# A hybrid decoder layer on one core: the first products of the up-projection put into a written order, with the norm of the second token half among them

## The chip, the core and the metric

The kernel runs on one core of a Trainium2 chip. Times are device microseconds (us) of one execution; lower is better. The engines are TensorE (PE, matrix products, with PEld for its weight loads), VectorE (DVE), ScalarE (ACT), GpSimd (POOL) and SyncE (SP, which issues every transfer here).

## What is computed

One step of a decoder layer: a mixer of Mamba-2 heads and sliding-window attention, then a convolutional feed-forward block. 1024 prompt tokens and 32 sample tokens go through the same weights, 1056 tokens in all. The part at issue is the feed-forward block:

```python
x = x + jnp.concatenate([y_ssd, y_att], axis=-1) @ lp['w_out']
hn = rmsnorm(x, lp['norm2'])
u, ffn_conv_new = causal_dwconv(hn @ lp['w_up'], ffn_conv_prev, lp['ffn_conv_w'], lp['ffn_conv_b'])
gate, val = jnp.split(u, 2, axis=-1)
x = x + (jax.nn.silu(gate) * val) @ lp['w_down']
```

with 1024 model columns, 2 x 2816 columns of `w_up` and a convolution over three tokens. `rmsnorm` scales each token by one over the root of its mean square.

## The kernel before

All operands of TensorE are split: a value is a high part (rounded, written by ScalarE with `act.activation(... Copy)`) and a low part (what the rounding left, written by VectorE as a subtraction), and a product takes high x high, high x low and low x high.

**Stages.** Input projection, mixers and the output projection come first (to 478 us of the profiled execution). The up-projection follows (478 to 949 us), then the down-projection. The up-projection's weights come in 22 pairs of 128 columns (a gate and a value block). Its tokens are two halves of 528 (`HT`), each of two quarters of 264 (`QC`).

**Seven products instead of eight.** For a pair and a half, `product(n, cp, tp, j)` with j = 0 to 6 makes the 2 x 2 block product by a seven-product scheme. `n` is a weight set, `cp` the pair, `tp` the half; j names which weight operand and which token operand it takes (`USES`: A11 with B11, S1 with T1, S2 with T2, A12 with B21, S4 with B22, S3 with T3, A22 with T4). One product is 12 matmuls of 128x264: four blocks of the contraction, three split terms each. A group is the seven products of one pair and half.

**Banks.** A group holds three PSUM banks, `bankof = "XZXYZXX"[j]`. X carries products 0, 2, 5 and 6 in a running sum, and each is read out before the next is added: 0, 2 and 6 by ScalarE, 5 by VectorE (`both(ub, ...)`, L996). So product 6 can't start before VectorE has read product 5. VectorE also reads products 3 (L1010) and 4 (L996).

**Token operands.** After the output projection of a half, `half_done` sums squares (`ssum`). `half_prep(tp)` calls `half_rstd`: twelve small matmuls with a column of ones (L851; six in the program, each in two passes), a Newton square root of fourteen tiny VectorE steps, six transposes (L858) and two ScalarE copies (L860). Then VectorE scales the half's eight blocks (L870, eight of 528 columns), forms differences (L887), and ScalarE and VectorE write seven operands, high (L882) and low (L883). B11 and T1 are needed first.

**Weight operands.** `up_load(n)` loads two raw tiles of 512 KB for weight set `n`; the pool has only two such tiles, so it waits until set n-1 is used up. `up_operand(n, j)` forms the weight operands: sums and differences (L922, L924, on VectorE for n < 3, on GpSimd from set 3 on), a high part (L934) and a low part (L935). There are eight operand tiles, so an operand of set n waits for a product of set n-1.

**Convolution.** `conv(cp, i)` runs when a pair's block is complete: ScalarE starts it (L1028), VectorE adds two shifted terms (L1030, 1072 columns each), ScalarE applies Silu (L1033, which needs another table), VectorE multiplies gate and value (L1039, L1040), and SP stores the result.

**Order.** `SETS` begins with pair 0 on half 0 (set 0), pair 1 on both halves (set 1), pair 0 on half 1 (set 2), pair 2 on both (set 3) and so on. Five groups are named here in the order of their need: G1 (pair 0, half 0), G2 (pair 1, half 0), G3 (pair 1, half 1), G4 (pair 0, half 1), then G5 and G6 (pair 2). G2.5 is product 5 of G2. No order is written by hand: a scheduler places each engine's instructions by its own estimate, and may put matmuls of several products among one another. `half_prep(1)` stands in the code behind all products of G1.

Of the kernel before, what the change touches and what calls it, by code (L numbers as in the profile page):

```python
# [46 lines left out]
def kernel(ctx, tc, xT, wxbc, wkv, wq, wz, wout, wup, wdn, cols, rows, cst, idm,  # L47
# [816 lines left out]

    def half_prep(tp):

        rb = half_rstd(tp)
# [8 lines left out]

        def operand(name, src):
            hl = [x2p[tp].tile([128, 4, QC], F32R, tag=name + p, name=f"x2{p}") for p in "hl"]
            X2[tp][name] = hl
            for j in range(2):  # L880
                h, l = (t[:, 2 * j:2 * j + 2] for t in hl)
                act.activation(out=h, in_=src[j], func=AF.Copy)  # L882
                dve.tensor_tensor(out=l, in0=src[j], in1=h.bitcast(F32), op=ALU.subtract)  # L883

        def minus(o, p, q):
            for j in range(2):
                dve.tensor_tensor(out=o[j], in0=p[j], in1=q[j], op=ALU.subtract)  # L887

        operand("B11", b11)
        minus(b11, b12, b11)  # L890
        operand("T1", b11)
        minus(b11, b22, b11)
        operand("T2", b11)
        operand("B21", b21)
        operand("B22", b22)
        minus(b12, b22, b12)
        operand("T3", b12)
        minus(b21, b21, b11)
        operand("T4", b21)

# [357 lines left out]
```

## Time and profile before

| what | us |
|---|---|
| median of 3 runs | 1204.72 (1203.46 to 1206.7) |
| the profiled execution's own time | 1208.17 |
| its span in the trace | 1206.4 |
| TensorE busy | 1161.6 (96%) |
| VectorE busy | 866.0 (72%) |
| ScalarE busy | 506.6 (42%) |
| GpSimd busy | 345.7 (29%) |

A busy TensorE is not one at its peak: matmuls overlap, so one that shows 0.28 us is followed by the next after 0.12 us. In the up-projection TensorE is without a gap from about 573 us on; what it waits for lies between 478 and 573 us.

### The profile page before, as it was taken

The page shows a single profiled execution, that of the slowest core. Times are in us where ns is not written, and L with a number is a line of the kernel's source. Part 1 is how long each engine was busy: PE and PEld are TensorE (multiplying, and loading weights), DVE is VectorE, ACT ScalarE, POOL GpSimd, SP SyncE. Part 2 cuts the span into 40 slices and gives each one's busy share as a digit, 9 for nine tenths or more (in the row PEclk, how much of TensorE's full clock was granted, in tenths as well). Part 3 has the DMA queues.
Part 4 walks back from the last instruction along what each step waited for, and adds up shares of the span by engine and source line. Part 5 has one row for each costly group of instructions (what it writes and reads, how often), then busy time and mean ns, then how long its engine had stood idle before and what let it go on. Part 6 is the DMA issues. An engine that isn't in the chain of part 4 may idle for free.

```text
span 1206.4 us, 22111 instructions
## 1 busy us (share of the span) xinstructions
PE 1161.6 (96%) x8614; PEld 1112.8 (92%) x8614; DVE 866.0 (72%) x1739; ACT 506.6 (42%) x992; POOL 345.7 (29%) x471
## 2 busy tenths in 40 slices
PE   7999999989989999888999999999999999999998
PEld 7998878869867999888999999999999999999998
DVE  7678857476686677897766676666666787777764
ACT  7444643444544344464545454545544322112110
POOL 0125445253444000044344343534343111001000
PEclk9999999999988899899999999999999999999999
DMA  8211112132645413113222222222222854323303
GB/s 291 63 62 57 36 32 75 29 84 79 184 144 164 169 71 131 43 54 106 87 75 81 80 72 80 72 80 71 89 72 89 336 174 145 121 89 119 102 9 145
DMA packets 52362, 122.53 MB, mean 102 GB/s; under 512 B 9233, under 2 KB 19985, under 8 KB 52241
## 3 DMA queue, kind: packets, MB, share of 16 engines
q1 hardware_dynamic: 52256, 121.12, 29.9%
q8 instruction: 67, 1.10, 0.4%
q14 instruction: 39, 0.31, 0.1%
HBM read 94.86 MB, written 27.26 MB: 101 GB/s over the span
## 4 chain that ended last, share of the span: by engine, by line
PE 82%; DVE 8%; DMA 5%; ACT 2%; issue 2%; POOL 1%; SPq 0%; POOLq 0%; DVEq 0%; ACTq 0%
PE ps L147 37%; PE ps L988 31%; PE ps L199 6%; DMA raw<-in_wup 2%; DVE au L935 1%; PE ps L525 1%; PE sc L503 1%; PE yy L653 1%; DVE x2l L883 1%; PE ps L517 1%; PE st L660 1%; DMA Cs<-ead 1%; DVE c L1030 1%; DMA xr<-in_xT 1%; PE ps L339 0%
## 5 line engine op out<-in xcount | busy, mean ns | idle before, releaser
L988 PE MATMUL ps<-x2h,au 128*128 128x264 f32 x2464 | 456.4, 286 | 10.6 <-ACT x2h L882 4.0
L988 PEld LDWEIGHTS ps<-x2h,au 128*128 128x128 f32 x2464 | 384.0, 189 | 13.2 <-ACT x2h L882 4.4
L988 PE MATMUL ps<-x2l,au 128*128 128x264 f32 x1232 | 348.8, 285 | 0.4 <-DVE x2l L883 0.4
L988 PEld LDWEIGHTS ps<-x2l,au 128*128 128x128 f32 x1232 | 232.5, 189 | 0.8 <-DVE x2l L883 0.8
L1103 DVE TENSOR_TENSOR acc<-acc,ps 128x352 f32<-128x352 f32 x264 | 131.1, 517 | 65.3 <-PE ps L147 64.7
L147 PE MATMUL ps<-xh,uh 128*128 128x264 f32 (+3 forms) x528 | 163.8, 318 | 10.1 <-ACT xh L182 5.6
L147 PE MATMUL ps<-gh,ul 128*128 128x352 f32 x528 | 170.1, 322 | 0.0
L147 PE MATMUL ps<-gl,uh 128*128 128x352 f32 x528 | 170.0, 322 | 0.0
L147 PE MATMUL ps<-gh,uh 128*128 128x352 f32 x528 | 167.9, 322 | 0.6 <-ACT gh L179 0.6
L147 PE MATMUL ps<-xl,uh 128*128 128x264 f32 (+3 forms) x528 | 166.2, 315 | 0.3 <-DVE xl L183 0.3
L147 PE MATMUL ps<-xh,ul 128*128 128x264 f32 (+3 forms) x528 | 165.4, 313 | 0.0
L116 ACT ACTIVATE uh<-raw 128x1024 fp32r<-128x1024 f32 (+3 forms) x59 | 55.9, 953 | 194.1 <-PE ps L147 173.7
L1030 DVE SCALAR_TENSOR_TENSOR c<-u,colt,c 128x1072 f32<-128x1072 f32 x88 | 119.9, 1364 | 3.6 <-ACT c L1028 3.5
L147 PEld LDWEIGHTS ps<-xh,uh 128*128 128x128 f32 x528 | 101.5, 195 | 14.5 <-ACT xh L182 6.6
L935 DVE TENSOR_TENSOR au<-raw,au 128x512 fp32r<-128x512 f32 x115 | 78.7, 700 | 39.9 <-ACT au L934 39.8
L147 PEld LDWEIGHTS ps<-xl,uh 128*128 128x128 f32 x528 | 102.8, 195 | 1.8 <-DVE xl L183 0.8
L147 PEld LDWEIGHTS ps<-xh,ul 128*128 128x128 f32 x528 | 102.8, 195 | 1.8 <-issue 1.0
L147 PEld LDWEIGHTS ps<-gh,uh 128*128 128x128 f32 x528 | 98.8, 188 | 0.9 <-ACT gh L179 0.9
L147 PEld LDWEIGHTS ps<-gl,uh 128*128 128x128 f32 x528 | 99.2, 188 | 0.4
L147 PEld LDWEIGHTS ps<-gh,ul 128*128 128x128 f32 x528 | 99.3, 188 | 0.0
L934 ACT ACTIVATE au<-raw 128x512 fp32r<-128x512 f32 x115 | 71.2, 625 | 34.8 <-PE ps L147 9.0
L935 DVE TENSOR_TENSOR au<-t,au 128x512 fp32r<-128x512 f32 x46 | 41.6, 904 | 36.0 <-PE ps L988 18.9
(295 smaller groups left out, 1936.8 us busy)
## 6 DMA issues: line engine op xcount, KB each, us to landing
raw<-in_wup SPq DMA_DIRECT2D x46, 512.0 KB, 3.6
gr<-gd SPq DMA_DIRECT2D x22, 528.0 KB, 4.8
gd<-c SPq DMA_DIRECT2D x22, 512.0 KB, 2.6
raw<-in_wdn SPq DMA_DIRECT2D x22, 512.0 KB, 4.1
raw<-in_wout SPq DMA_DIRECT2D x12, 512.0 KB, 3.5
acc<-in_xT SPq DMA_DIRECT2D x16, 264.0 KB, 5.3
accd<-acc SPq DMA_DIRECT2D x16, 264.0 KB, 2.1
acc<-accd SPq DMA_DIRECT2D x8, 528.0 KB, 8.2
```

Of the source, the lines that this page charges most:

```text
L116: act.activation(out=hi, in_=raw, func=AF.Copy)
L147: pe.matmul(out=ps, lhsT=w(a, k), rhs=x(b, k), start=first and k == ks[0] and i == 0, stop=last and k == ks[-1] and i == 2)
L199: pe.matmul(out=ps[:m, :n], lhsT=x[k][c][:, a:a + m], rhs=w[k // nk][b][:, o:o + n], start=k == 0 and i == 0, stop=k == 7 and i == 2)
L503: pe.matmul(out=sb[:, v, c].rearrange("p i k -> p (i k)"), lhsT=qT[a][r, c], rhs=kT[b][r, o:o + 256], start=i == 0, stop=i == 2)
L517: pe.transpose(out=pt[:, h], in_=P[:, h], identity=ident)
L525: pe.matmul(out=po[64 * v:64 * v + 64, 0:256].rearrange("p (c q) -> p c q", c=2), lhsT=(vall[:, t - i] if i or not t else vdif[:, t - 1])[ ...
L653: pe.matmul(out=o, lhsT=xw[:, c], rhs=M[:, 2 * i + h], start=True, stop=not off)
L934: act.activation(out=u[:, 0:512], in_=src, func=AF.Copy)
L935: dve.tensor_tensor(out=u[:, 512:1024], in0=src, in1=u[:, 0:512].bitcast(F32), op=ALU.subtract)
L988: pe.matmul(out=ps, lhsT=wgt[:, 512 * a + 128 * k:512 * a + 128 * k + 128], rhs=xx[b][:, k], start=opens and k == 0 and i == 0, stop=k == ...
L1030: dve.scalar_tensor_tensor(out=c[:, 0:n], in0=u[:, j:j + n], scalar=col(C_FW + 3 * m + j), in1=c[:, 0:n], op0=ALU.mult, op1=ALU.add)
L1103: dve.tensor_tensor(out=o, in0=o, in1=ps[:, :PC], op=ALU.add)
```

## The change

TensorE's instructions of the whole up-projection keep the order in which they are written (`in_order`, a region for TensorE alone). A second region does the same for VectorE and ScalarE through the first four groups. In it every step is written out by hand: products, scalings of the second half's blocks, high and low parts of token and weight operands. For that `half_prep` is cut into `scale`, `high` and `low`, `up_operand` into `up_high` and `up_low`. `half_rstd(1)` now stands behind the second product of G1 and `half_bcast(1, ...)` (transposes and copies) behind its fourth. Products of one group stand between those of the next: product 6 of a group comes behind two or more products of the group after it. Behind the region the code has set 3's operands, the three convolutions of pairs 1 and 0, and then the loop as before; these follow the scheduler's order on VectorE and ScalarE, and it may place them among the region's instructions.

```diff
     def half_rstd(tp):
         ...
         rsqrt(pt_, v[:88, 1], v[:88, 0], 88, 6)
+        return v
+
+    def half_bcast(tp, v):
         for q in range(2):
         ...
-    def half_prep(tp):
-
-        rb = half_rstd(tp)
-        for m in (4, 5, 6, 7, 0, 1, 2, 3):
+    def half_prep(tp, rb):
+
+        def scale(m):
             h = half(m, tp)
             dve.scalar_tensor_tensor(out=h, in0=h, scalar=col(C_N2 + m), in1=rb, op0=ALU.mult, op1=ALU.mult)
         ...
+        def high(name, j):
+
+            if name not in X2[tp]:
+                X2[tp][name] = [x2p[tp].tile([128, 4, QC], F32R, tag=name + p, name=name + p + "xy"[tp]) for p in "hl"]
+            o, *d = FROM[name]
+            if d:
+                dve.tensor_tensor(out=o[j], in0=d[0][j], in1=d[1][j], op=ALU.subtract)
+            act.activation(out=X2[tp][name][0][:, 2 * j:2 * j + 2], in_=o[j], func=AF.Copy)
+
+        def low(name, j):
+            h, l = (t[:, 2 * j:2 * j + 2] for t in X2[tp][name])
+            dve.tensor_tensor(out=l, in0=FROM[name][0][j], in1=h.bitcast(F32), op=ALU.subtract)
         ...
-    def up_operand(n, j):
+    def up_high(n, j):
         ...
+    def up_low(n, j):
+        u, src = A[n, j]
         dve.tensor_tensor(out=u[:, 512:1024], in0=src, in1=u[:, 0:512].bitcast(F32), op=ALU.subtract)
         ...
-    last = None
+    in_order = tc.manual_schedule(engines={mybir.EngineType.PE})
+    in_order.__enter__()
+
+    with tc.manual_schedule(engines={mybir.EngineType.DVE, mybir.EngineType.Activation}):
+        up_load(1)
+        product(0, 0, 0, 0)
+        product(0, 0, 0, 1)
+        v1 = half_rstd(1)
+        product(0, 0, 0, 2)
+        product(0, 0, 0, 3)
+        scale, high, low = half_prep(1, half_bcast(1, v1))
+        up_high(1, 0)
+        scale(4)
+        up_low(1, 0)
+        up_high(1, 1)
+        product(0, 0, 0, 4)
         ...
+        product(1, 1, 0, 5)
+        high("B22", 0)
+        low("B21", 1)
+        high("B22", 1)
+        low("B22", 0)
+        product(1, 1, 1, 0)
+        product(1, 1, 1, 1)
+        low("B22", 1)
+        high("T2", 0)
+        product(1, 1, 0, 6)
         ...
+        product(2, 0, 1, 5)
+    up_load(3)
+    for j in range(7):
+        up_operand(3, j)
+    conv(1, 0)
+    conv(1, 1)
+    conv(0, 0)
+    last = (2, 0, 1), True
     for n, (cp, groups) in enumerate(SETS):
-        for g in groups:
+        for g in groups if n > 2 else ():
         ...
-            if g == (0, 0):
-                half_prep(1)
     product(*last[0], 6)
     conv(last[0][1], 1)
+    in_order.__exit__(None, None, None)
```

The order of TensorE in the region is G1.0 to G1.5, G2.0, G2.1, G1.6, G2.2 to G2.5, G3.0, G3.1, G2.6, G3.3, G3.2, G3.4, G3.5, G4.0, G4.1, G3.6, G4.2 to G4.5; behind it G5.0, G5.1, G4.6, G5.2 to G5.5, G6.0, G6.1, G5.6 and so on. Three places follow as the built programs have them. Names end in a buffer number. `acc` are the half's blocks, `au` weight operands (in the changed kernel `aua` to `aug` for j = 0 to 6), `x2h` and `x2l` token operands (now named, as `B11ly`, with x for half 0 and y for half 1), `u` the products' sums, `c` convolutions.

Place 1, VectorE, the scalings of the second half. Before, with G2's products 3, 4 and 5 read at L1010 and L996:

```order
L935 TENSOR_TENSOR au_5962<-raw_5944,au_5962 128x512
L1010 TENSOR_TENSOR u_5842<-u_5842,ps_5904 128x264
L924 TENSOR_TENSOR t1_5993<-raw_5945 128x512
L996 TENSOR_TENSOR u_5842<-s2_5902,ps_5862 128x264
L870 SCALAR_TENSOR_TENSOR acc_5111<-acc_5111,colt_84,ssum2_5166 128x528 x2
L870 SCALAR_TENSOR_TENSOR acc_5225<-acc_5225,colt_84,ssum2_5166 128x528 x2
L870 SCALAR_TENSOR_TENSOR acc_5346<-acc_5346,colt_84,ssum2_5166 128x528 x2
L870 SCALAR_TENSOR_TENSOR acc_5473<-acc_5473,colt_84,ssum2_5166 128x528 x2
L996 TENSOR_TENSOR u_5845<-s5_5875,ps_5848 128x264
L883 TENSOR_TENSOR x2l_5793<-acc_5111,x2h_5792 128x528
```

Now, from the last step of the square root on, with G1's products 3, 4 and 5 read at L1024 and L1010:

```order
L140 SCALAR_TENSOR_TENSOR v2_5683<-rs_5685 88x6
L1024 TENSOR_TENSOR u_5641<-u_5641,ps_5712 128x264
L872 SCALAR_TENSOR_TENSOR acc_5111<-acc_5111,colt_84,ssum2_5166 128x528
L945 TENSOR_TENSOR aua_5736<-raw_5637,aua_5736 128x512
L930 TENSOR_TENSOR t1_5740<-raw_5638 128x512
L1010 TENSOR_TENSOR u_5641<-s2_5710,ps_5661 128x264
L872 SCALAR_TENSOR_TENSOR acc_5111<-acc_5111,colt_84,ssum2_5166 128x528
L945 TENSOR_TENSOR aub_5742<-t1_5740,aub_5742 128x512
L928 TENSOR_TENSOR t1_5740<-t1_5740,raw_5637 128x512
L1010 TENSOR_TENSOR u_5644<-s5_5674,ps_5647 128x264
```

and, some rows on, up to the reading of G2.5 (the row of `u_5782`):

```order
L888 TENSOR_TENSOR acc_5225<-acc_5225 128x2x264
L893 TENSOR_TENSOR T1ly_5857<-acc_5111,T1hy_5856 128x528
L945 TENSOR_TENSOR aug_5861<-raw_5638,aug_5861 128x512
L1024 TENSOR_TENSOR u_5779<-u_5779,ps_5871 128x264
L893 TENSOR_TENSOR T1ly_5857<-acc_5225,T1hy_5856 128x528
L872 SCALAR_TENSOR_TENSOR acc_5346<-acc_5346,colt_84,ssum2_5166 128x528 x2
L1010 TENSOR_TENSOR u_5779<-s2_5854,ps_5804 128x264
L872 SCALAR_TENSOR_TENSOR acc_5473<-acc_5473,colt_84,ssum2_5166 128x528
L893 TENSOR_TENSOR B21ly_5889<-acc_5346,B21hy_5888 128x528
L872 SCALAR_TENSOR_TENSOR acc_5473<-acc_5473,colt_84,ssum2_5166 128x528
L1010 TENSOR_TENSOR u_5782<-s5_5817,ps_5785 128x264
```

The eight scalings stood in one run behind G2's readings; now they begin among G1's and are spread over G1 and G2, with set 1's weight operands between them.

Place 2, VectorE, the reading of G3.5 (`u_5845`, L996) before:

```order
L996 TENSOR_TENSOR u_5842<-s2_6010,ps_5965 128x232
L998 TENSOR_TENSOR u_5842<-s2_6010,ps_5965 128x8x4
L935 TENSOR_TENSOR au_6066<-raw_5944,au_6066 128x512
L1010 TENSOR_TENSOR u_5637<-u_5637,ps_6162 128x264
L996 TENSOR_TENSOR u_5845<-s5_5978,ps_5948 128x232
L998 TENSOR_TENSOR u_5845<-s5_5978,ps_5948 128x8x4
L935 TENSOR_TENSOR au_6048<-raw_5944,au_6048 128x512
L935 TENSOR_TENSOR au_6069<-raw_5945,au_6069 128x512
L1030 SCALAR_TENSOR_TENSOR c_6074<-u_5842,colt_84,c_6074 128x1072 x2
```

and now (`u_5782`, L1010):

```order
L945 TENSOR_TENSOR aub_6019<-t1_6017,aub_6019 128x512
L888 TENSOR_TENSOR acc_5473<-acc_5473,acc_5225 128x2x264
L893 TENSOR_TENSOR T4ly_6022<-acc_5346,T4hy_6021 128x528
L928 TENSOR_TENSOR t1_6017<-t1_6017,raw_5867 128x512
L1044 SCALAR_TENSOR_TENSOR c_6207<-u_5779,colt_84,c_6207 128x1072
L893 TENSOR_TENSOR T4ly_6022<-acc_5473,T4hy_6021 128x528
L1010 TENSOR_TENSOR u_5782<-s5_5954,ps_5927 128x232
L1012 TENSOR_TENSOR u_5782<-s5_5954,ps_5927 128x8x4
L945 TENSOR_TENSOR auc_6044<-t1_6017,auc_6044 128x512
L928 TENSOR_TENSOR raw_5867<-raw_5867,raw_5868 128x512
L945 TENSOR_TENSOR aud_6062<-raw_5867,aud_6062 128x512
L1044 SCALAR_TENSOR_TENSOR c_6207<-u_5779,colt_84,c_6207 128x1072
```

The two convolution steps of pair 1's gate block stood behind set 2's last weight operands; now one stands ahead of the reading of G3.5, the other ahead of the last three of those operands.

Place 3, TensorE, where set 3's second weight operand is first used. Before, `ps_6245` is G5.1, `ps_6298` G5.3, and `ps_6359` and `ps_6342` are G6.1 and G6.0:

```order
L988 MATMUL ps_6245<-x2h_5069,au_6141 128x264
L988 MATMUL ps_6245<-x2l_5070,au_6141 128x264
L988 MATMUL ps_6359<-x2h_5800,au_6141 128x264
L988 MATMUL ps_6359<-x2l_5801,au_6141 128x264
L988 MATMUL ps_6298<-x2h_5083,au_6176 128x264
L988 MATMUL ps_6298<-x2l_5084,au_6176 128x264
L988 MATMUL ps_6342<-x2h_5792,au_6097 128x264
L988 MATMUL ps_6342<-x2l_5793,au_6097 128x264
```

and now, the end of G5.0 and the start of G5.1:

```order
L1002 MATMUL ps_6236<-B11lx_5062,aua_6179 128x264
L1002 MATMUL ps_6236<-B11hx_5061,aua_6179 128x264
L1002 MATMUL ps_6250<-T1hx_5067,aub_6184 128x264
L1002 MATMUL ps_6250<-T1lx_5068,aub_6184 128x264
L1002 MATMUL ps_6250<-T1hx_5067,aub_6184 128x264 x2
```

Matmuls of four products stood among one another; now each product stands whole and in its place.

## Rows read from the trace of the kernel before

**Rows 1.** The page: span, and busy time, share and instructions of engines.

```profile
span 1206.4 us, 22111 instructions
PE 1161.6 (96%) x8614; PEld 1112.8 (92%) x8614; DVE 866.0 (72%) x1739; ACT 506.6 (42%) x992; POOL 345.7 (29%) x471
```

**Rows 2.** Windows, L988 alone: stretch, length, PE busy, PEld busy, clock, DMA, GB/s.

```profile
477.98:487.98 10.00, 9.27 (x75) 9.09 (x76) 1.00 0.39 122
...
497.98:507.98 10.00, 5.76 (x27) 5.04 (x26) 0.66 0.01 2
...
577.98:677.98 100.00, 100.00 (x821) 100.00 (x821) 1.00 0.24 81
```

**Rows 3.** Waits of TensorE, 478 to 600 us: total, times, longest.

```profile
PE ps L988 <- ACT x2h L882: 4.0, 2, 2.3
PE ps L988 <- ACT au L934: 3.3, 2, 1.7
PE ps L988 <- DVE u L996: 1.3, 2, 1.0
PE ps L988 <- DVE au L935: 1.1, 2, 0.6
PE ps L988 <- DVE u L998: 0.6, 1, 0.6
PE ps L988 <- DVE x2l L883: 0.4, 1, 0.4
PE ps L988 <- ACT s L1008: 0.2, 1, 0.2
```

**Rows 4.** Timeline of VectorE: start, us, what, count, idle before and its releaser.

```profile
430.74 0.16 DVE L853 TENSOR_SCALAR v<-ps 88x6 f32<-88x6 f32 x1 [1.19 <-PE ps L851]
...
432.90 0.16 DVE L140 SCALAR_TENSOR_TENSOR v<-rs 88x6 f32<-88x6 f32 x1
...
435.57 5.53 DVE L870 SCALAR_TENSOR_TENSOR acc<-acc,colt,ssum 128x528 f32<-128x528 f32 x8 [1.36 <-ACT ssum L860]
...
490.92 1.28 DVE L935 TENSOR_TENSOR au<-raw,au 128x512 fp32r<-128x512 f32 x2
...
497.73 0.42 DVE L996 TENSOR_TENSOR u<-s,ps 128x264 f32<-128x264 f32 x1
498.07 5.52 DVE L870 SCALAR_TENSOR_TENSOR acc<-acc,colt,ssum 128x528 f32<-128x528 f32 x8
...
503.84 3.18 DVE L883 TENSOR_TENSOR x2l<-acc,x2h 128x528 fp32r<-128x528 f32 x5
...
524.36 2.70 DVE L1030 SCALAR_TENSOR_TENSOR c<-u,colt,c 128x1072 f32<-128x1072 f32 x2
...
533.99 2.32 DVE L1039 TENSOR_TENSOR c<-c 128x1024 f32<-128x1024 f32 x1
...
546.61 1.21 DVE L1039 TENSOR_TENSOR c<-c 128x1024 f32<-128x1024 f32 x1
```

**Rows 5.** Timeline of GpSimd, a weight operand's steps, set 3 and set 4.

```profile
533.56 1.68 POOL L922 TENSOR_TENSOR t<-t,raw 128x512 f32<-128x512 f32 x1 [0.86 <-DVE au L935]
...
551.81 1.28 POOL L924 TENSOR_TENSOR t<-raw 128x512 f32<-128x512 f32 x1 [13.08 <-DMA raw<-in_wup]
```

**Rows 6.** Timeline of ScalarE: table load, Silu, and a weight operand's high part.

```profile
528.05 1.28 ACT L1033 ACT_TABLE_LOAD   x1
529.35 1.10 ACT L1033 ACTIVATE c<-c 128x1072 f32<-128x1072 f32 x1
...
548.94 0.63 ACT L934 ACTIVATE au<-raw 128x512 fp32r<-128x512 f32 x1 [4.58 <-DMA raw<-in_wup]
```

**Rows 7.** The raw weight tiles, 475 to 600 us: times from issue to landing.

```profile
DMA to landing us min/median/max: 3.5/4.6/5.5
```

**Rows 8.** Timeline of TensorE: first half's transposes, then the down-projection's first matmuls.

```profile
434.43 0.62 PE L858 MATMUL ps<-idt,v 88*128 88x88 f32 x6
...
946.26 1.39 PE L147 MATMUL ps<-gh,uh 128*128 128x352 f32 x7 [0.65 <-ACT gh L179]
```

More of the change, by code (lines that the diff above doesn't have):

```diff
@@ L875, in half_prep, with half_prep_all @@
         b11, b12, b21, b22 = quarter(0, 0), quarter(0, 1), quarter(1, 0), quarter(1, 1)
-        def operand(name, src):
-            hl = [x2p[tp].tile([128, 4, QC], F32R, tag=name + p, name=f"x2{p}") for p in "hl"]
-            X2[tp][name] = hl
+        FROM = {"B11": (b11,), "T1": (b11, b12, b11), "T2": (b11, b22, b11), "B21": (b21,), "B22": (b22,),
+                "T3": (b12, b22, b12), "T4": (b21, b21, b11)}
+        def high(name, j):
[8 more added lines that the diff above has]
+            dve.tensor_tensor(out=l, in0=FROM[name][0][j], in1=h.bitcast(F32), op=ALU.subtract)
+        return scale, high, low
+    def half_prep_all(tp, rb):
+        scale, high, low = half_prep(tp, rb)
+        for m in (4, 5, 6, 7, 0, 1, 2, 3):
+            scale(m)
+        for name in ("B11", "T1", "T2", "B21", "B22", "T3", "T4"):
             for j in range(2):
[L881 to L885, printed above, removed]
+                high(name, j)
             for j in range(2):
[L887 to L899, printed above, removed]
+                low(name, j)
     SETS = [(0, [(0, 0)]), (1, [(1, 0), (1, 1)]), (0, [(0, 1)])]
@@ L943 @@
         half_done(m, 0, m == 0)
-    half_prep(0)
+    half_prep_all(0, half_bcast(0, half_rstd(0)))
     for i, m in enumerate((4, 5, 6, 7, 0, 1, 2, 3)):
@@ L1043, in conv @@
         del U[cp]
-    last = None
+    in_order = tc.manual_schedule(engines={mybir.EngineType.PE})
[13 more added lines that the diff above has]
+        product(0, 0, 0, 4)
+        scale(5)
+        up_low(1, 1)
+        up_high(1, 2)
+        product(0, 0, 0, 5)
+        scale(6)
+        up_low(1, 2)
+        up_high(1, 3)
+        product(1, 1, 0, 0)
+        scale(7)
+        up_low(1, 3)
+        up_high(1, 4)
+        product(1, 1, 0, 1)
+        high("B11", 0)
+        up_low(1, 4)
+        up_high(1, 5)
+        low("B11", 0)
+        product(0, 0, 0, 6)
+        high("B11", 1)
+        up_low(1, 5)
+        product(1, 1, 0, 2)
+        high("T1", 0)
+        low("B11", 1)
+        up_high(1, 6)
+        high("T1", 1)
+        low("T1", 0)
+        up_low(1, 6)
+        up_load(2)
+        product(1, 1, 0, 3)
+        low("T1", 1)
+        scale(0)
+        scale(1)
+        high("B21", 0)
+        product(1, 1, 0, 4)
+        scale(2)
+        low("B21", 0)
+        scale(3)
+        high("B21", 1)
+        product(1, 1, 0, 5)
[8 more added lines that the diff above has]
+        product(1, 1, 0, 6)
+        high("T2", 1)
+        low("T2", 0)
+        low("T2", 1)
+        product(1, 1, 1, 3)
+        high("T3", 0)
+        up_high(2, 0)
+        high("T3", 1)
+        low("T3", 0)
+        product(1, 1, 1, 2)
+        up_low(2, 0)
+        low("T3", 1)
+        up_high(2, 1)
+        high("T4", 0)
+        product(1, 1, 1, 4)
+        up_low(2, 1)
+        high("T4", 1)
+        low("T4", 0)
+        up_high(2, 2)
+        low("T4", 1)
+        product(1, 1, 1, 5)
+        up_low(2, 2)
+        up_high(2, 3)
+        product(2, 0, 1, 0)
+        up_high(2, 5)
+        up_low(2, 3)
+        product(2, 0, 1, 1)
+        up_high(2, 4)
+        up_low(2, 5)
+        product(1, 1, 1, 6)
+        up_high(2, 6)
+        up_low(2, 4)
+        product(2, 0, 1, 2)
+        up_low(2, 6)
+        product(2, 0, 1, 3)
+        product(2, 0, 1, 4)
+        product(2, 0, 1, 5)
@@ L1050 @@
                 up_load(n + 1)
-            done = n >= 2 if cp == 0 else g[1] == 1
             for j in range(6):
                 product(n, *g, j)
-                if j == 1 and last:
+                if j == 1:
                     product(*last[0], 6)
@@ L1061 @@
                 up_operand(n + 1, 6)
-            if done:
+            if g[1]:
                 conv(cp, 0)
-            last = (n, *g), done
-            if g == (0, 0):
-                half_prep(1)
+            last = (n, *g), g[1] == 1
     product(*last[0], 6)
     conv(last[0][1], 1)
+    in_order.__exit__(None, None, None)
     sp.dma_start(out=fco, in_=fcot)
```

6 lines of the change are left out of this document (5 added, 1 removed).

## The prediction, made before the changed kernel was run

> **What bounds the kernel now.** The page comes first: TensorE is busy for 1161.6 us of a span of 1206.4, VectorE for 866.0 [rows 1]. So a step of another engine counts only where TensorE stands for it. The windows say what undisturbed products cost: 821 matmuls in 100.00 us, 0.1218 us each, so 12 x 0.1218 = 1.46 us for a product [rows 2]. TensorE's waits, listed for 478 to 600 us, are then what the change can win: 4.0 + 3.3 + 1.3 + 1.1 + 0.6 + 0.4 + 0.2 = 10.9 us [rows 3]. The largest is for high parts of token operands, which are late because VectorE scales the second half only from 498.07 on, 20.1 us after the first product's first matmul at 477.98, in one run of 5.52 us [rows 4]. In that stretch TensorE was also granted a clock of only 0.66 (a part of it at 1.2 instead of 2.4 GHz): 27 matmuls in 10 us are 3.3 us of work, 6.7 are lost, and with 4.2 of these as waits (2.3 + 1.7 of the two longest, and the 0.2) about 2.5 go to the clock [rows 2, 3]. At stake are thus 10.9 + 2.5 = 13.4 us, 1.1%. Times below are "+t", from the first matmul of G1.0.
>
> **The norm moved forward.** The work is the same, only its place is new. The small matmuls with ones hold up TensorE before as after: in the first 10 us 75 matmuls ran where 82 fit, 10 - 75 x 0.1218 = 0.9 us [rows 2]; transposes that show 0.62 us for six [rows 8] I put at 0.4. Both cancel in the difference. The norm's VectorE chain ran from 430.74 to 432.90 + 0.16 for the first half, 2.3 us [rows 4]; the two products G1.2 and G1.3 (2.92 us) cover it, and if they did not, the price would be the chain's remainder, below 1 us. From transposes to first scaling it was 435.57 - 434.43 = 1.1 us [rows 4, 8]. So the first scaling starts at 2 x 1.46 + 0.9 + 2 x 1.46 + 1.0 = about +7.7 instead of +20.1. That is the gain that the change can draw on: 12.4 us of head start.
>
> **What fixed order makes of it: G2.6.** X is one bank, so G2.6 waits until VectorE has read G2.5, and that reading now stands behind everything written ahead of it. From the first scaling to it there are in the order (place 1) 8 scalings at 0.68 (5.53 / 8), 11 weight steps at 0.60, 7 token steps (low parts, differences) at 0.62 and 5 readings at 0.34 (498.07 - 497.73) [rows 4]: 5.4 + 6.6 + 4.3 + 1.7 = 18.1 us. Some low parts must await ScalarE's high part of 0.63 [rows 6]; I take 0.8 for that, between 0 and one such step for two of them. 7.7 + 18.1 + 0.8 = +26.6. TensorE has done the 15 products ahead of G2.6 at 15 x 1.46 + 0.9 + 0.4 = +23.2. It waits 3.4 us (2.6 without the 0.8; 3.7 with 1.1 of it).
>
> **G3.6.** From there to the reading of G3.5 VectorE has 15 token steps at 0.62, 4 weight steps at 0.60, readings of 0.34 + 2 x 0.41 (a second small one goes with some) and, as place 2 shows, a convolution step of 1.25 (half of 2.70, less the overlap) [rows 4]: 9.3 + 2.4 + 1.2 + 1.25 = 14.1, with 0.3 for handing over +41.0. TensorE goes on from +26.6 with seven products: 10.2, +36.8. It waits 4.2 us (3.2 if the convolution step came later, 4.6 with a second wait for ScalarE). A half clock after the first wait would be swallowed by this one, since VectorE sets its end.
>
> **Set 3.** Its raw tiles come into the places of set 2's, so the load waits for the last step that reads these. The products after G3.6 bring TensorE to 41.0 + 5 x 1.46 = +48.3, where G5.0 wants set 3's first operand. VectorE finishes the three weight steps and one convolution step behind the reading at 41.0 + 3 x 0.60 + 1.25 = +44.05. ScalarE then stands at a table load (1.28) and Silu (1.10), which the scheduler may place here, until about +45.9; a high part 0.63 and low part 0.60 end at +47.2 [rows 4, 6]. A raw tile needs 4.6 us at the median [rows 7]: +51.8, and the high part +52.4. TensorE waits 4.1 us (3.0 if Silu comes later, 4.6 with the slowest transfer). Before, TensorE could fill such a gap with matmuls of other products (place 3); now it can't. Next G5.1 needs S1 = a sum of both tiles. The second tile's load goes out some 0.8 us after the first's, +48.0, and lands with 5.5 at +53.4 [rows 7]; GpSimd takes 1.28 [rows 5] and the high part 0.63: +55.4, its low part 0.6 more, against G5.1's start at +53.9. That is 2.0 us (0.8 with the median transfer, 2.6 with a slow GpSimd step). G5.2 may wait too (0 to 2.0); I take 0, as GpSimd's next step begins when S1's does end.
>
> **G5.6.** The reading of G5.5 stands on VectorE behind the low part of set 4's first operand, which hangs on a load that goes out once set 3's tiles are free: about +61.5, + 4.6, + 0.63 + 0.69 = +67.4 [rows 6, 7]. A reading, a product of gate and value (1.21) and the reading itself follow: 0.34 + 1.14 + 0.1 + 0.34 brings +69.3. The product of gate and value took 1.21 us alone and 2.32 beside GpSimd's step at 533.56 of 1.68 [rows 4, 5], so 1.1 comes on top: +70.4. TensorE gets there after nine products from +52.4 and the wait of 2.0, at +67.6, and waits 2.8 (0.5 to 3.5).
>
> A page gives a reason for the 2.32. The Trainium skill, "SBUF — State Buffer", section "Who interferes with whom", says that a VectorE instruction with two inputs in SBUF and a GpSimd instruction that reads SBUF exclude each other for their whole length. By that rule VectorE would have stood until 535.24 (533.56 + 1.68) and ended 1.21 later, 2.46 us after its start; the trace has 2.32, near enough. With rule or row the sum holds 1.1 at G5.6; without any collision it would be 15.4 instead of 16.5.
>
> **What else changes.** Down at the end of the up-projection, the last product 6 now comes behind more work: in the trace of before TensorE stood 0.65 us ahead of the first 128x352 matmuls [rows 8], and the change has 21 instead of 7 of them in front of the part that needs the last pair. I take 0.65 as a gain (0 to 0.65). Loads by SP: the set 1 load is issued where it was needed anyway; nothing waits for it that the timeline shows. The half clock of 2.5 us I leave where it was: one wait of 4 us remains after the change as before, at G5.0, with a bound of 2.5 either way.
>
> **Sum.** Waits after: 3.4 + 4.2 + 4.1 + 2.0 + 2.8 = 16.5. Before: 10.9. 16.5 - 10.9 - 0.65 = +4.95. On the profiled execution's 1208.17 us that is 1213.1; that execution lies 3.45 above the median of the three runs (1204.72), and against this I forecast 1204.72 + 4.95 = **1209.7**. From the low and high ends, with not all at one end at once, +2 to +8.5: 1207 to 1213.
>
> **Rivals.** A measurement of this kernel can tell some 0.3% from no change, 3.6 us: 1201.1 to 1208.3.
>
> *No change.* The total work of VectorE up to set 3 stays, and only its order differs. If the places at set 3 and G5.6 cost what before cost outside the token operands and the last 0.2 (10.9 - 4.0 - 0.4 - 0.6 - 0.2 = 5.7) because the early waits gave the loads time, then 3.4 + 4.2 + 5.7 - 10.9 - 0.65 = +1.75: 1206.5. For it speaks that a later TensorE finds later loads landed; against it that the loads hang on the same VectorE chain that makes TensorE late. 0.32 with the lower part of the forecast, 0.22 without.
>
> *Faster.* VectorE is not behind, and the waits at G2.6 and G3.6 vanish. It decides by one point: the reading of G2.5 must be issued by +23.2. The 31 steps would have 15.5 us, 0.50 each, where the rows make 18.1, 0.58. Yet if the first scaling came at +5 (the chain beside only one product) and ScalarE never was late, 23.1 would do. Then 5.7 - 10.9 - 0.65 = -5.85, and with 2.7 more or 2.5 less (loads as in my sum; clock regained) -2.7 to -8.4: about 1199. Chance 0.17.
>
> *Much slower.* From 573 us on TensorE had no gap, with an order that the scheduler could mix. Now each product must be read in time at its own place. Were it 0.3 us late in each of the 38 groups that follow, 38 x 0.3 = 11.4 more: 1221. For it: VectorE is 72% busy [rows 1]. Against it: the readings that gate a product come once in 10.2 us per group, and VectorE works some 7 of these. 0.07.
>
> That the change doesn't do what it says is excluded by the order: the scalings stand among G1's readings, and TensorE's products stand whole.
>
> **Numbers.** The forecast has 0.54, of which 0.10 lies below 1208.3; no change 0.22, faster 0.17, much slower 0.07. So faster 0.17, same 0.22 + 0.10 = 0.32, slower 0.44 + 0.07 = 0.51. The range from 1199.0 to 1214.5 leaves out half of the faster case (0.09), the much slower one (0.07) and a rest of the forecast (0.04).
>
> **What would show it.** The first scaling near +7.7: if at +5 or +10, G2.6's wait moves with it. TensorE waiting for VectorE's reading of G2.5 and G3.5 (L1010), 3.4 and 4.2 us; 0 there makes the faster rival right. A wait for set 3's high part (L940), 4.1, behind a table load and Silu on ScalarE. 2.0 at G5.1, and 2.8 at G5.6 with the product of gate and value (L1053) near 2.3. No idle time of TensorE after some +75; if there is some in every group, the last rival. A clock below 1.00 in the windows around +23 to +41 without a longer wait behind it would be a term that the sum lacks. And the sum fails as a whole if the VectorE steps, next to GpSimd or not, take other times than the 0.60 to 0.68 of the rows.

## The result, and the profile after

The changed kernel took 1214.62 us (median of 6 runs, 1212.56 to 1215.9) beside 1207.51 us of the kernel before on the same occasion (6 runs): a ratio of 1.0064 [1.0044, 1.0083]; that is 7.7 us by the ratio, which is one of means, and 7.1 between the medians. Later it was run twice more, on other chips: 1.0039 [1.0020, 1.0058] and 1.0030 [1.0015, 1.0045] (e12 and e9 below). The mean of the three is 1.0044, or 5.3 us, against the forecast of 4.95; that these are so near is luck, as the terms of the sum show further down. The forecast time of 1209.7 was low for two reasons of like size: the kernel before stood 2.8 us above the median that the forecast was built on, and the first measurement of the ratio was the highest of three.

The page of the changed kernel, profiled execution of 1212.56 us, span 1210.8 us:

```profile
PE 1164.0 (96%) x8614; PEld 1117.3 (92%) x8614; DVE 866.1 (72%) x1739; ACT 503.4 (42%) x992; POOL 337.5 (28%) x471
```

VectorE does the same work as before [rows 1]. Next, TensorE's waits from 470 to 620 us (total, times, longest), which answer to [rows 3]:

```profile
PE ps L1002 <- DVE u L1010: 4.4, 2, 3.1
PE ps L1002 <- DVE u L1012: 2.4, 1, 2.4
PE ps L1002 <- ACT aua L940: 2.1, 1, 2.1
PE ps L1002 <- ACT aub L940: 1.4, 1, 1.4
PE ps L1002 <- DVE aub L945: 0.7, 1, 0.7
PE ps L1002 <- ACT s L1022: 0.6, 1, 0.6
PE ps L1002 <- DVE aua L945: 0.2, 1, 0.2
```

The releasers have changed: no token operand (4.0 + 0.4 us before) is waited for any more, but VectorE's readings of G2.5, G3.5 and G5.5, and set 3. The sum is 11.8 instead of 10.9 us. Where they stand shows TensorE's timeline (start, length, instruction, idle before and its releaser), with the first and the last matmul:

```profile
476.40 0.28 PE L1002 MATMUL ps<-B11hx,aua 128*128 128x264 f32 x1
...
503.90 0.59 PE L1002 MATMUL ps<-T4hx,aug 128*128 128x264 f32 x1 [3.12 <-DVE u L1010]
...
519.77 0.44 PE L1002 MATMUL ps<-T4hy,aug 128*128 128x264 f32 x1 [2.38 <-DVE u L1012]
...
530.96 0.39 PE L1002 MATMUL ps<-B11hx,aua 128*128 128x264 f32 x1 [2.10 <-ACT aua L940]
...
534.61 0.39 PE L1002 MATMUL ps<-T1hx,aub 128*128 128x264 f32 x1 [1.44 <-ACT aub L940]
...
550.50 0.39 PE L1002 MATMUL ps<-T4hx,aug 128*128 128x264 f32 x1 [1.29 <-DVE u L1010]
...
949.22 1.82 PE L147 MATMUL ps<-gh,uh 128*128 128x352 f32 x7 [2.01 <-ACT gh L179]
...
1206.96 0.32 PE L147 MATMUL ps<-gh,ul 128*128 128x352 f32 x1
```

T4 marks a product 6: G2.6 starts at 503.90 - 476.40 = +27.5, G3.6 at +43.4, G5.0 at +54.6, G5.1 at +58.2, G5.6 at +74.1. From there to the down-projection TensorE has no gap. From the first product to the last matmul it is 1206.96 - 476.40 = 730.56 us; in the kernel before the last matmul starts at 1202.56, so 724.58 us. That is 6.0 more in this pair of executions: 0.9 of waits in the up-projection, 1.4 at the start of the down-projection (2.0 against 0.65), and 3.7 that no wait explains. In the first 130 us TensorE started 919 matmuls of the up-projection before and 890 now (stretch, length, TensorE busy, clock, DMA share, GB/s; first the kernel before):

```profile
477.98:607.98 130.00, 118.02 (x919) 0.97 0.22 75
```

```profile
476.40:606.40 130.00, 117.02 (x890) 0.95 0.22 75
```

29 fewer at 0.1218 are 3.5 us; with 0.9 of it as waits some 2.6 are left. Most of that is the clock: it is granted at 0.64 and 0.67 behind G2.6, for example, where the kernel before has one such stretch [rows 2]. The rest of the 3.7 lies mostly at the start of the down-projection, where the clock is 0.66 for 5 us in the changed kernel and 1.00 before. Behind G2.6:

```profile
501.40:506.40 5.00, 2.50 (x11) 2.50 (x12) 0.64 0.08 30
506.40:511.40 5.00, 5.00 (x31) 5.00 (x30) 0.67 0.00 0
```

(stretch, length, TensorE busy, weight loads busy, clock, DMA share, GB/s). VectorE's timeline answers to [rows 4]: the first scaling, the readings of G2.5 and G3.5, the convolution step ahead of the latter, a weight operand's low part that waits for ScalarE behind its table load and Silu, and the product of gate and value.

```profile
484.35 0.77 DVE L872 SCALAR_TENSOR_TENSOR acc<-acc,colt,ssum 128x528 f32<-128x528 f32 x1 [0.43 <-ACT ssum L863]
...
503.43 0.42 DVE L1010 TENSOR_TENSOR u<-s,ps 128x264 f32<-128x264 f32 x1
...
517.28 1.32 DVE L1044 SCALAR_TENSOR_TENSOR c<-u,colt,c 128x1072 f32<-128x1072 f32 x1
...
519.15 0.38 DVE L1010 TENSOR_TENSOR u<-s,ps 128x232 f32<-128x232 f32 x1
...
524.74 0.69 DVE L945 TENSOR_TENSOR aue<-raw,aue 128x512 fp32r<-128x512 f32 x1 [0.85 <-ACT aue L940]
...
547.86 2.14 DVE L1053 TENSOR_TENSOR c<-c 128x1024 f32<-128x1024 f32 x1
```

The scalings begin at +8.0 instead of +20.1, and yet TensorE now waits for VectorE's readings. The windows say why. First the kernel before, then the changed one, the first 50 us in tens; columns are length, busy time and instructions of TensorE, weight loads, VectorE, ScalarE and GpSimd, then clock, DMA share and GB/s:

```profile
477.98:487.98 10.00, 10.00 (x89) 10.00 (x88) 5.80 (x11) 4.42 (x9) 0.60 (x4) 1.00 0.39 122
487.98:497.98 10.00, 10.00 (x86) 10.00 (x86) 7.48 (x24) 4.41 (x10) 0.00 (x0) 1.00 0.27 105
497.98:507.98 10.00, 5.76 (x27) 5.04 (x26) 10.00 (x17) 4.34 (x8) 0.00 (x0) 0.66 0.01 2
507.98:517.98 10.00, 9.62 (x77) 9.13 (x75) 10.00 (x18) 7.21 (x14) 0.00 (x0) 1.00 0.00 1
517.98:527.98 10.00, 9.39 (x73) 8.96 (x73) 9.96 (x19) 6.05 (x10) 3.90 (x5) 1.00 0.29 104
```

```profile
476.40:486.40 10.00, 10.00 (x91) 10.00 (x90) 6.27 (x21) 3.69 (x9) 0.61 (x4) 1.00 0.38 122
486.40:496.40 10.00, 9.39 (x78) 9.18 (x77) 9.15 (x16) 5.25 (x12) 0.00 (x0) 1.00 0.00 0
496.40:506.40 10.00, 6.88 (x47) 6.66 (x46) 9.60 (x17) 4.66 (x9) 0.00 (x0) 0.82 0.35 107
506.40:516.40 10.00, 9.89 (x69) 9.68 (x68) 9.13 (x17) 5.91 (x11) 1.31 (x2) 0.84 0.01 2
516.40:526.40 10.00, 7.62 (x51) 7.43 (x50) 9.04 (x15) 7.43 (x13) 1.30 (x2) 0.83 0.00 0
```

5.80 + 7.48 + 10.00 + 10.00 + 9.96 = 43.2 us before, and 6.27 + 9.15 + 9.60 + 9.13 + 9.04 = 43.2 after. In 50 us VectorE did no more work, though it could start 12 us earlier: what it gained by +20 (2.1 us) it lost in small waits of the written order by +50.

### The profile page after: what moved, and what is told of

Read it like the earlier page. It is cut to its first block, busy times and chain, and to the rows that moved or that the text cites. A ratio compares the mean times of both kernels' runs of the same rounds, so it can differ in the third digit from the quotient of the medians.

```text
span 1210.8 us, 22103 instructions
## 1 busy us (share of the span) xinstructions
PE 1164.0 (96%) x8614; PEld 1117.3 (92%) x8614; DVE 866.1 (72%) x1739; ACT 503.4 (42%) x992; POOL 337.5 (28%) x471
## 4 chain that ended last, share of the span: by engine, by line
PE 86%; DVE 6%; DMA 3%; ACT 2%; issue 1%; POOL 1%; SPq 0%; POOLq 0%; ACTq 0%
PE ps L147 38%; PE ps L1002 33%; PE ps L199 6%; PE ps L525 1%; PE sc L503 1%; DMA Cs<-ead 1%; PE yy L653 1%; PE two L147 1%; DMA raw<-in_wup 1%; PE ps L517 1%; PE st L660 1%; DMA gr<-gd 1%; PE yy L655 0%; PE ps L339 0%; POOL pt L520 0%
## 5 line engine op out<-in xcount | busy, mean ns | idle before, releaser
L119 DVE TENSOR_TENSOR ul<-raw,uh 128x1024 fp32r<-128x1024 f32 (+3 forms) x51 | 58.7, 1158 | 9.3 <-ACT uh L116 9.3
L199 PE MATMUL ps<-uh,xh 128*128 128x256 f32 (+3 forms) x216 | 61.1, 283 | 0.6 <-DVE dtr L363 0.4
L199 PE MATMUL ps<-uh,xl 128*128 128x256 f32 (+3 forms) x216 | 61.0, 283 | 0.0
L199 PE MATMUL ps<-ul,xh 128*128 128x256 f32 (+3 forms) x216 | 60.7, 283 | 0.0
L1042 ACT ACTIVATE c<-u,colt 128x1072 f32<-128x1072 f32 x44 | 56.0, 1272 | 0.1
L945 DVE TENSOR_TENSOR auc<-t,auc 128x512 fp32r<-128x512 f32 x23 | 24.3, 1057 | 42.0 <-ACT auc L940 42.0
L928 POOL TENSOR_TENSOR t<-t,raw 128x512 f32<-128x512 f32 x20 | 26.2, 1310 | 99.8 <-DVE aub L945 99.8
```

Source lines behind the costliest of these rows:

```text
L119: (e or dve).tensor_tensor(out=lo[:, i:i + n], in0=raw[:, i:i + n], in1=hi[:, i:i + n].bitcast(F32), op=ALU.subtract)
L199: pe.matmul(out=ps[:m, :n], lhsT=x[k][c][:, a:a + m], rhs=w[k // nk][b][:, o:o + n], start=k == 0 and i == 0, stop=k == 7 and i == 2)
L928: minus = lambda o, p, q: e.tensor_tensor(out=o, in0=p, in1=q, op=ALU.subtract)
L1042: act.activation(out=c[:, 0:n], in_=u[:, 0:n], func=AF.Identity, scale=col(C_FW + 3 * m), bias=col(C_FB + m))
```

## The experiments

Three theories stood against each other. A: VectorE's work up to a milestone (a time at which TensorE needs a reading or an operand) decides. B: TensorE's written order loses the time, since it can't fill a wait. C: the half clock behind the waits is the loss. Ratios are to the kernel before on the same chip. Milestones are counted from each run's first product.

**e4, VectorE's work taken away.** In `scale`, `if tp: return` ahead of the instruction.

> The changed kernel without the eight scalings of the second half (its blocks go on unscaled), which takes 8 x 0.68 = 5.4 us from VectorE. Theory A (VectorE's sum): the reading of G2.5 comes at +21.6 instead of +27.0, ahead of TensorE; no wait at G2.6, under 0.5 us at G3.6, set 3 some 4 us earlier; with the half clock gone 6 to 9 us below the changed kernel, at or under the kernel before. Theory B (the fixed order): under 2 us.

Ratio 0.9984 [0.9967, 1.0002]. That is 0.0060 below the mean of the changed kernel's three ratios, some 7 us, as A expected. G2.6 waits for nothing. G3.6:

```profile
514.59 0.36 PE L1004 MATMUL ps<-T4hy,aug 128*128 128x264 f32 x1 [2.40 <-DVE u L1014]
```

514.59 - 476.4 = +38.2, so 5.2 us earlier for 5.4 us of VectorE's work. TensorE still waits 2.4 there, and not under 0.5, as it is earlier too. A holds for the milestone nearly one to one. (The second half's operands also hang on no norm in this run.)

**e3, the order ahead of a milestone changed, not the work.**

```diff
-        scale(0)
-        scale(1)
-        high("B21", 0)
         product(1, 1, 0, 4)
-        scale(2)
         ...
         product(1, 1, 0, 5)
+        scale(0)
+        scale(1)
+        high("B21", 0)
+        scale(2)
         ...
```

> The changed kernel with the scalings of blocks 0 to 3 and the steps of B21 written behind the reading of G2.5 instead of ahead of it. Theory A (VectorE's sum): the reading of G2.5 comes some 3 us earlier and G2.6 waits for nothing, but G3.3, which needs B21, waits as long; G3.6 starts as before, at +43; within 1 us of the changed kernel. Theory C (the wait at G2.6 and the half clock behind it are what is lost): 3.1 us of wait and some 2 us of clock go, 3 to 5 us below.

Ratio 1.0039 [1.0021, 1.0057]. The wait at G2.6 is gone, others for B21 and T2 are there instead (the largest 1.67), and G3.6 starts at 521.92 - 478.8 = +43.1 against +43.4:

```profile
521.92 0.36 PE L1002 MATMUL ps<-T4hy,aug 128*128 128x264 f32 x1 [1.26 <-DVE u L1012]
```

As A has it; the time is that of e12 too.

**e6, the clock held.** Matmuls that nobody reads: 24 ahead of G2.6, 18 ahead of G3.6.

```diff
+        warm(24)
         product(1, 1, 0, 6)
         ...
+        warm(18)
         product(1, 1, 1, 6)
```

> The changed kernel with 24 matmuls of 128x264 whose result nobody reads ahead of G2.6 (24 x 0.12 = 2.9 us) and 18 ahead of G3.6 (2.2 us), so that TensorE has work while it waits for VectorE. Theory A (VectorE's sum): the ends of both waits stay where they are, at +27.5 and +43.4; if the clock is then granted in full behind them, the loss behind G2.6 was swallowed by the wait at G3.6 anyway, and only the loss between G3.6 and G5.0 turns into a longer wait at G5.0: within 1.5 us of the changed kernel. Theory C (the half clock is a loss of its own): 2 to 4 us below it.

Ratio 1.0040 [1.0016, 1.0064].

```profile
500.76 0.39 PE L1002 MATMUL ps<-T4hx,aug 128*128 128x264 f32 x1 [0.24 <-DVE u L1010]
...
515.96 0.36 PE L1002 MATMUL ps<-T4hy,aug 128*128 128x264 f32 x1 [0.22 <-DVE u L1012]
...
547.52 0.55 PE L1002 MATMUL ps<-T4hx,aug 128*128 128x264 f32 x1 [2.53 <-DVE u L1010]
```

From 473.3: +27.5, +42.7 and, at G5.6, +74.2. The clock is full from +25 to +50, and falls behind set 3's waits instead:

```profile
498.25:523.25 25.00, 22.60 (x172) 1.00 0.04 11
523.25:533.25 10.00, 6.57 (x34) 0.69 0.39 149
```

The milestones stay, and so does the time. So C falls for the stretch from G2.6 to set 3: its half clock lies for the most part inside the next wait. What the half clock behind set 3 costs, no run has tested.

**e7, differences on GpSimd.** `e = dve if n < 1 else pool` instead of `n < 3`.

> The changed kernel with the sums and differences of sets 1 and 2 on GpSimd, as those of set 3 on: eight steps of 0.60 leave VectorE, and GpSimd, idle from 482 to 515 us, has 8 x 1.28. If GpSimd's steps don't hold VectorE up: VectorE's milestones at G2.6, G3.6 and G5.0 come 2.4, 4.8 and 4.8 us earlier, 4 to 7 us below the changed kernel. If they exclude each other as the product of gate and value with GpSimd's step (2.14 and 2.32 against 1.21): 8 x (1.28 - 0.60) = 5.4 us later, up to 5 us above it.

Ratio 1.0056 [1.0036, 1.0077].

```profile
505.93 0.39 PE L1002 MATMUL ps<-T4hx,aug 128*128 128x264 f32 x1 [4.15 <-DVE u L1010]
...
522.03 0.36 PE L1002 MATMUL ps<-T4hy,aug 128*128 128x264 f32 x1 [3.29 <-DVE u L1012]
```

From 476.7: +29.2 and +45.3, 1.7 and 1.9 later although eight steps had left VectorE. One pair of steps side by side:

```profile
489.05 1.63 POOL L928 TENSOR_TENSOR raw<-raw 128x512 f32<-128x512 f32 x1
```

```profile
489.67 1.56 DVE L945 TENSOR_TENSOR auc<-t,auc 128x512 fp32r<-128x512 f32 x1
```

This low part takes 0.68 in the changed kernel, and five VectorE steps beside GpSimd's are longer by 0.9 to 1.1 each up to G3.6. The trace agrees with the rule that the Trainium skill gives in "SBUF — State Buffer", section "Who interferes with whom": the steps of the two engines exclude each other. It is not the only cause: VectorE also stands 2.06 us instead of 0.70 for the high part of set 1's fifth operand, which now waits for GpSimd's step.

**e2, the convolutions kept out.** The three `conv` calls of pairs 1 and 0 moved to the end of the written region.

> The changed kernel with the three convolutions of pairs 1 and 0 written into the region, behind the reading of G4.5, so that no convolution step and no Silu stands ahead of the reading of G3.5 or of set 2's weight operands. Theory A (VectorE's sum): G3.6 starts 1.2 us earlier, set 3's load goes out some 3 us earlier (two steps of 1.25 and ScalarE's 0.85), G5.0 and G5.1 wait under 1 us: 2 to 4 us below the changed kernel. Theory B (the fixed order): the lateness moves to where the convolutions now stand; within 1 us of the changed kernel.

Ratio 1.0031 [1.0012, 1.0050].

```profile
539.50 0.59 PE L1002 MATMUL ps<-T2hx,auc 128*128 128x264 f32 x1 [2.40 <-ACT auc L940]
```

G3.6 is 1.3 earlier (520.38 - 478.3 = +42.1) and G5.0 3.8 earlier (+50.8), as A expected, but the wait then comes at G5.2, behind ScalarE's table load and Silu, which now stand there. Of the expected 2 to 4 us the ratio shows none that stands clear of e12.

**e1 and e13, TensorE's written order ended behind G4.5.** Run with the changed kernel on one chip as e12 and e13.

```diff
         product(2, 0, 1, 5)
+    in_order.__exit__(None, None, None)
     up_load(3)
     ...
     conv(last[0][1], 1)
-    in_order.__exit__(None, None, None)
```

> The changed kernel, but TensorE's written order ends behind G4.5: from G5 on the scheduler orders TensorE again. Theory A (VectorE's sum): VectorE is full from the first scaling (+8) to set 3's weights, so the waits at G2.6 (3.1 us) and G3.6 (2.4) stay, and of the 5.7 us behind them (2.1 + 0.2 at G5.0, 1.4 + 0.7 at G5.1, 1.3 at G5.6) half stays, since few other products have operands then; with 1 to 3 us from the start of the down-projection: 2 to 4 us below the changed kernel's 1214.6. Theory B (the fixed order): the 5.7 us of waits, some 2 us of half clock behind them and the 2.8 us at the start of the down-projection go: 9 to 10 us below, at or under the kernel before.

> The changed kernel itself, once more, beside the next two runs on one chip. e9 turned out to have the changed kernel's order on every engine and measured 1.0030 where the changed kernel measured 1.0064. If both are draws of one thing: 1.003 to 1.006. Its waits ahead of G2.6 and G3.6 end at +27.5 and +43 as before, whatever the clock.

> e1 again, on the same chip as the changed kernel. Theory A (VectorE's sum): the released order from G5 on is worth 1 to 3 us, since VectorE's milestones stay and only the start of the down-projection and a part of set 3's waits move. Theory B (the fixed order is the main loss): 5 us or more between the two.

e1 has 1.0014 [0.9996, 1.0031], e13 1.0006 [0.9992, 1.0020], e12 on e13's chip 1.0039 [1.0020, 1.0058]: 4.0 us between the two on one chip, more than A's 1 to 3, less than B's 5. G2.6 starts at +27.5 in all, G3.6 at +42.7 to +43.4. So most of the change's 5.3 us hangs on the order that is written behind the first four groups. The waits at G2.6 and G3.6 are still there in e1 and e13, and most of the loss is gone. With TensorE's order released the scheduler also places some steps of VectorE, ScalarE and GpSimd otherwise, so it needn't be TensorE's order alone. Which places of the order it is, the traces don't settle: the waits of the up-projection are 11.8, 13.7 and 12.8 us in three executions of the changed order, 11.9 and 11.0 in e1 and e13; the start of the down-projection 2.0, 1.4 and 0 against 0.65 twice; from the first product to the last matmul the two orders differ by 2.7 us in the mean of three and two executions.

**e9, the last product released.** `in_order` ended ahead of the last product 6.

> The changed kernel with TensorE's written order ending ahead of the very last product 6 of the up-projection, so that the scheduler may place it among the first matmuls of the down-projection. If the written order is what makes the start of the down-projection wait (2.0 us and some 1.4 of half clock against 0.65 before): the wait falls to 0.6 and 2 to 3 us go against the changed kernel. If the later load of the first gated block does it: the wait stays at 1.5 to 2 us, within 1 us.

Ratio 1.0030 [1.0015, 1.0045]; but every engine's instructions stand as in the changed kernel, so it says nothing on the released product. It is a repetition, and shows what repeats:

```profile
502.54 0.39 PE L1002 MATMUL ps<-T4hx,aug 128*128 128x264 f32 x1 [3.13 <-DVE u L1010]
...
517.73 0.36 PE L1002 MATMUL ps<-T4hy,aug 128*128 128x264 f32 x1 [2.40 <-DVE u L1012]
```

```profile
501.40:506.40 5.00, 3.44 (x25) 1.00 0.01 3
506.40:511.40 5.00, 4.02 (x30) 1.00 0.00 0
```

The same wait at the same +27.5, and this time the full clock behind it. G3.6 starts at 517.73 - 475.0 = +42.7, only 0.7 earlier than at half clock.

**e5, the early norm alone, in the kernel before.** `half_rstd(1)` behind the second product of G1 and the transposes behind the fourth; no written order.

> The kernel before with one part of the change alone: the ones-matmuls and square root of the second half written behind the second product of G1, transposes and copies behind its fourth; no written order on any engine. Theory A (VectorE's sum is the bound, not the start of the scalings): the scalings start some 5 us earlier, but set 1's weight operands then stand behind them or between; TensorE's waits from 478 to 573 us stay at 9 to 12 us; within 2 us of the kernel before. Rival (the late norm is what the kernel before lost): the 4.0 us of waits for token operands and 2 us of half clock go, 4 to 6 us below the kernel before.

Ratio 0.9997 [0.9978, 1.0016]. The early norm alone does nothing that can be measured. In its one trace TensorE's waits are 6.9 us, not the 9 to 12 expected (2.7 of them still for token operands); but the stage from the first product to the last matmul is only 1.7 us shorter (722.9 against 724.6), as the time outside waits grew.

**e14, the kernel before without the second half's scalings.** The loop over its eight blocks is skipped; so its operands hang on no norm.

> The kernel before without the eight scalings of the second half (its blocks go on unscaled, so its operands also hang on no norm). This is the most that any earlier norm could give the kernel before, and 5.4 us of VectorE besides. Theory A (VectorE's sum): most of the 10.9 us of waits and the 2.5 us of half clock come from VectorE being full from +20 to +50, so 5 to 9 us go. Rival (the waits come from loads and products anyway): under 3 us.

Ratio 0.9907 [0.9885, 0.9929], 11 us less, more than the 5 to 9 expected. VectorE is now nearly full in the first 20 us (9.71 and 10.00, where the kernel before had 5.80 and 7.48), and the clock is 1.00:

```profile
474.30:484.30 10.00, 9.47 (x78) 9.26 (x77) 9.71 (x17) 9.13 (x19) 2.55 (x4) 1.00 0.38 122
484.30:494.30 10.00, 10.00 (x87) 9.79 (x86) 10.00 (x21) 5.17 (x11) 0.00 (x0) 1.00 0.00 0
```

So the lateness of the second half costs the kernel before nearly all that was at stake (13.4 us). It is worth having, but it takes less work of VectorE, or other work in its first 20 us, and not only an earlier start. It can't be said which of the two, since this run has both. Beside e4 it shows something more: both kernels lack the same eight steps, and the written order is then 0.9984 against 0.9907, some 9 us slower. VectorE's sum doesn't explain that; the written order itself has a price.

**e8, three things together**: e3's and e1's edits, and set 3's operands in the region with their differences on VectorE.

> Three things together: the scalings of blocks 0 to 3 and B21 behind the reading of G2.5 (as one run before); set 3's operands inside the region, their sums and differences on VectorE, pair 1's convolution steps ahead of the reading of G4.4 and its Silu and the other convolutions behind set 3's last operand; TensorE's written order ends behind G4.5. Theory A (VectorE's sum): each takes work from ahead of a milestone, so the gains add: 3.6 of the released order, 2.5 of the scalings, and 3 to 5 of set 3's waits, 8 to 11 us below the changed kernel, 1 to 4 below the kernel before. Rival (the waits only move to the next place, G6 and pair 3): no further than the released order alone, 1209 to 1210.

Ratio 1.0040 [1.0023, 1.0057]: worse than the released order alone. G5.0 comes at 529.98 - 478.4 = +51.6 instead of +54.6, but then product 2, which needs bank X, waits until ScalarE has read product 0 of its group, and that reading stands behind set 3's seven high parts, the table load, Silu and two convolutions (at 543.92). The rival was right that the wait only moves to the next place; the time is above its 1209 to 1210.

```profile
544.34 0.39 PE L1002 MATMUL ps<-T2hx,auc 128*128 128x264 f32 x1 [2.40 <-ACT u L1016]
```

**e10 and e11, other groups first.** Pair 2 on both halves between pair 1's halves, in the kernel before; e11 with e5's edit too.

```diff
-    SETS = [(0, [(0, 0)]), (1, [(1, 0), (1, 1)]), (0, [(0, 1)])]
+    SETS = [(0, [(0, 0)]), (1, [(1, 0)]), (2, [(2, 0), (2, 1)]), (1, [(1, 1)]), (0, [(0, 1)])]
```

> The kernel before with another order of groups: pair 2 on half 0 and then on half 1 stands between pair 1's two halves (sets: pair 0, pair 1, pair 2, pair 1 again, pair 0 again), and the preparation of the second half behind pair 1's group. It needs one set of weight operands more (7 x 0.60 + 4 x 0.60 = 6.6 us on VectorE), but the second half is needed 10.2 us later and no convolution falls ahead of the third half-1 group. Theory A (VectorE's sum up to each milestone decides): with 10.2 us more of TensorE's products ahead of the second half's first use, VectorE's 20 us of preparation fit; the 4.0 us of waits for token operands and most of the half clock go, the waits at the next sets stay: 2 to 6 us below the kernel before. Rival (the sum is the same by the end of the sixth group, so the waits come there): within 2 us.

> As the run before it, with the ones-matmuls and the square root of the second half behind the second product of the first group, and its transposes and copies behind the fourth. Theory A: the preparation has slack already, so the early norm adds nothing: within 1 us of the run before it. Rival (the start of the scalings matters): 2 us or more below it.

Ratios 1.0054 [1.0035, 1.0074] and 1.0061 [1.0039, 1.0082]. Neither expectation of e10 came true; e11 lies within 1 us of it, as A has it. The second half is needed later, and VectorE is late for it still (4.6 us of waits for its low parts); that the additional weight set ahead of it is the cause is argued, not shown:

```profile
PE ps L988 <- DVE x2l L883: 4.6, 3, 1.9
```

No version that computes everything beat the kernel before.

## Why the prediction was right, and where it was wrong

**Right.** The direction, and the first steps. The first scaling came at +8.0 (forecast +7.7), G2.6 at +27.5 (+26.6) after 3.1 us (3.4), G5.1 after 2.1 (2.0), and no wait followed G5.6. The product of gate and value took 2.14 us (2.3). The claim that a half clock behind G2.6 is swallowed at G3.6 is borne out by the changed kernel beside e9 but for 0.7 us. The much slower rival fell with the missing gaps behind +75; the faster one because VectorE read G2.5 at +27, not by +23.2.

**Wrong, TensorE's pace behind a wait.** This step failed: "TensorE goes on from +26.6 with seven products: 10.2, +36.8", and in the same way five products at 1.46 behind G3.6, with "The half clock of 2.5 us I leave where it was". The seven products took 13.5 us, with a clock of 0.64 and 0.67 up to 511.40, so TensorE reached G3.6 only at 519.77 - 2.38 - 476.40 = +41.0; the five took 9.1 instead of 7.3, with a mean clock of 0.83 in the ten us around them. Time that the forecast put into the waits went into slower matmuls ahead of them. The waits sum to 11.8 us in this execution (to 13.7 in others), not 16.5: 2.4 at G3.6 (4.2), 2.3 at G5.0 (4.1), 1.3 at G5.6 (2.8), with 0.6 for ScalarE's reading that the sum lacks. Outside the waits some 2.6 us more were lost than before, where the sum had nothing.

VectorE was late as well, at +43.4 instead of +41.0. Its term of 14.4 us measured 15.9; most of the rest went to waits (0.37, 0.58 and smaller) that a sum of durations leaves out. The two errors partly cancel in a wait, and show in full in the milestone: each was forecast too early, by 0.9, 2.4, 2.2 and 3.7 us.

**Luck in the sum.** Against the kernel before, the forecast has +5.6 of waits, 0 of clock and -0.65 at the down-projection, +4.95 in all. This pair of executions has +0.9 of waits, some +2.6 outside them and the rest of its +6.0 at the down-projection. The total is near because errors cancel. Of the waits the rival *no change* had the better figure: it put 5.7 us on set 3 and G5.6, and 2.1 + 0.2 + 1.4 + 0.7 + 1.3 = 5.7 came. And e1 and e13 keep the waits at G2.6 and G3.6 without most of the loss, so the waits that the forecast added up are not what the change costs; where the loss sits behind the fourth group stays open.

**Wrong, the start of the down-projection.** A gain of 0.65 was put in; there were losses of 1.4 and 0.8 and once a gain of 0.65. In these three executions ScalarE stands for the first gated block's load, issued by SP at 941.44 here and in e12 at 944.07, with ScalarE's high part behind it at 948.09 and 948.43:

```profile
941.44 1.45 SPq L1203 DMA_DIRECT2D gr<-gd  x2
...
948.09 1.08 ACT L179 ACTIVATE gh<-gr 128x1056 fp32r<-128x1056 f32 x1 [3.86 <-DMA gr<-gd]
```

It took 6.7 us here, 4.4 in e12. In the kernel before the same step follows ScalarE's work without a gap, so the forecast had no term for the load. Whether the order of the last product counts there, no run has tested.

**The absolute time.** The upper end of the range lay 9.8 us above a median of three runs; the kernel before then measured 2.8 higher and the change 7.1 above that, so 1214.62 lies 0.1 us above 1214.5. The range had width for the steps of the sum, none for the base moving.

## What to carry to other kernels

When a chain of small steps is moved forward, first add up what the engine that executes what follows has to do by each time at which another engine needs a result. An earlier start buys only the idle time that it fills and keeps; here VectorE worked 43.2 us of the first 50 before and after. In a sum of waits, count what comes behind each wait too: here TensorE went on at half clock, and the next wait was shorter for it. A written order should end where it was worked out: released behind the fourth group, the same kernel lost 0.7 us instead of 4.7 on one chip.

## What the runs showed of the hardware that was not expected

The granted clock behind one and the same wait is not the same in each execution: behind 3.12 us at G2.6 it was 0.64 to 0.67 for 10 us, behind 3.13 us in e9, with every instruction in the same place, 1.00. Profiled executions of one program differ accordingly: from the first product to the last matmul 730.6, 728.4 and 726.4 us in three of the changed kernel. Against the 724.6 of the one trace of before that is 1.8 to 6.0 us: a single pair of traces could not have told this change from one of a third of its size.
